# A decoder layer on one core: operands of the norm requested earlier, the second phase's pools in another order, the gate's finished rows two steps apart

## The chip, the cores and the metric

The kernel runs on one core of one Trainium2 chip. The metric is device microseconds of one execution, from its first to its last instruction with what lies around them; less is better. Engines are called as the profile calls them: PE (TensorE), DVE (VectorE), ACT (ScalarE), POOL (GpSimd), SP (SyncE, which here only issues transfers).

## The reference, cut to what matters

One decoder layer over 2048 tokens of width 1024, all in float32:

```python
u = _rmsnorm(h, ln1_g); proj = u @ w_in               # 3088 columns
...                                                   # gated linear attention, short convolution
h = h + concatenate([o, y]) @ w_out
u2 = _rmsnorm(h, ln2_g)
a, bb = split(u2 @ w_gate_upffn)                      # 2 x 2816 columns
h = h + (silu(a) * bb) @ w_down
u3 = _rmsnorm(h, ln3_g)
gate = sigmoid(u3 @ w_ple_gate)                       # 1024 x 1024
h = h + gate * (p @ w_ple_proj)                       # p: 2048 x 256, the embeddings
return _rmsnorm(h, lnf_g)
```

## The kernel before, in words

A float32 product is three fast matmuls: each operand is split into a rounded high part (a cast on ACT, L105 or L162) and a rest (a subtraction on DVE, L106 or L163), and high x high, high x rest and rest x high are summed. The three large products with `w_gate_upffn`, `w_down` and `w_ple_gate` are cut into blocks and made with seven block products in place of eight; the left operands of the seven are sums and differences of a first and a second half of the tokens' operands. They lie in DRAM as `up_1` to `up_7`, `u3_1` to `u3_7` and `hid_1` to `hid_7`.

There are three phases, each with pools of its own on the same SBUF addresses, given out in the order in which the pools are named. A tile of the next phase that lies where a tile of the phase before lay waits for the last use of that one.

- **Mixing phase** (0 to about 957 us): four blocks `b` of 512 tokens, each of `NT` = 4 tiles of 128 tokens. Only the order of PE's work is written by hand; the other engines' order is set by a scheduler. Near the end of a block each tile gets its residual, is stored (`h_mid<-w`, L670), normed (`normed`), transposed and written out by `norm_to_ops`. In blocks 0 and 2 this writes `up_1` and `up_2`. In blocks 1 and 3 (tile >= NT) it reads those two back (`old`, two loads, L232), makes four differences on POOL (L218, 128x512 each) and stores `up_3` to `up_7` (L235). After block 3 the embeddings of the first two blocks are multiplied with `w_ple_proj` (`embedding`): ACT copies the results (L725) and POOL issues their stores (`emb<-w`, L727).
- **Up phase** (to about 1870 us), order by hand. It opens with two loads of the other embeddings `p` (`ur<-in_p_dram`, L865), two of `w_ple_proj` (L869), splits them, turns `p` on PE (L267), and makes 16 embedding products (matmuls `mm<-U,U`, their stores L903) before the up product starts. Beside these, `fetch_U` loads the first `up_` operands (L280) and L790 the first weights. The SP queue runs its transfers in order; a transfer whose tile isn't free holds up all behind it.
- **Last phase**: the down product twice, then the gate for the first half of the tokens, `gated(0)`, and for the second, `gated(1)`, which is final. A step is twelve matmuls of 512 columns; `then(n, fn)` runs `fn` n steps later. A job is two steps; its two loads (`wr`, `mr`, L1023) are issued some jobs ahead, and its casts `wh`, `mh` (L162) two ahead. In `gated(0)` a finished row of 128 tokens goes through `finish`: POOL adds the residual with an accumulating transfer (`h<-h_out`, L1251), ACT squares it into a tile of the pool `w4` (L1107), POOL makes the inverse root, DVE scales (L1126) into the same tile, SP stores it (`out_dram<-w`, L1247). `w4` has four tiles here, so that the fifth row's squares wait until the first row's store has landed. ACT runs in order too: what waits there holds up the casts behind it. These steps of the eight rows of `gated(0)` fall into the first ones of `gated(1)`, whose own rows are loaded meanwhile (`row`, `h<-h_out` on SP, L1231).

Of the kernel before, what the change touches and what calls it, by code (L numbers as in the profile page):

```python
# [14 lines left out]
P = 128  # L15
# [4 lines left out]
NT = T // P  # L20
# [19 lines left out]
def hybrid_layer(ctx: ExitStack, tc: tile.TileContext,  # L40
                 x, p, ln1_g, w_in, w_gate_up, b_gate, conv_w, gn_g, w_out, ln2_g,
                 w_up, w_down, ln3_g, w_pg, w_pp, lnf_g, out):
    nc = tc.nc
    x, out = x[0], out[0]
# [9 lines left out]
    def tile_of(tag):  # L54
        return lambda shape, dt=F32: pl[tag].tile(shape, dt, name=tag)

    big, w4, t2 = tile_of("uT"), tile_of("w4"), tile_of("t2")
# [6 lines left out]
    def pools(stack, spec, space=None):  # L64
        for tag, bufs in spec.items():
            kw = {} if space is None else {"space": space}
            pl[tag] = stack.enter_context(tc.tile_pool(name=tag, bufs=bufs, reuse_waits="tile", **kw))
# [70 lines left out]
    def later(n, fn):  # L138
        queue.append((clock[0] + n, fn))
        queue.sort(key=lambda e: e[0])  # L140
# [30 lines left out]
    def tok_of(ti):  # L171
        return slice(ti * P, (ti + 1) * P)
# [3 lines left out]
    def rstd_of(src, dst):  # L176

        ss = tiny.tile([P, 1], F32, name="ss")
        nc.scalar.activation(out=dst, in_=src, func=AF.Square, scale=1.0 / 32.0, accum_out=ss)
        ms = tiny.tile([P, 1], F32, name="ms")  # L180
        nc.gpsimd.tensor_scalar(out=ms, in0=ss, scalar1=EPS, scalar2=None, op0=ALU.add)
        rs = tiny.tile([P, 1], F32, name="rs")
        last["rs"] = nc.gpsimd.tensor_tensor(out=rs, in0=ms, in1=mhalf[:, 0:1], op=ALU.pow)
        return rs
# [8 lines left out]
    def normed(src, gain):  # L193
        xn = w4([P, D])
        rs = rstd_of(src, xn)
        nc.vector.scalar_tensor_tensor(out=xn, in0=src, scalar=rs, in1=gain, op0=ALU.mult, op1=ALU.mult)
        return xn

    def transposed(xn, kk):
        tp = tr_bank().rearrange("p (a b) -> p a b", b=P)  # L200
        for a in range(4):
            c = (kk * 4 + a) * P
            nc.tensor.transpose(out=tp[:, a, :], in_=xn[:, c:c + P], identity=ident)
        return tp
# [12 lines left out]
    def tensor(e, out, a, b, op):  # L217
        return e.tensor_tensor(out=out, in0=a, in1=b, op=op)  # L218

    def norm_to_ops(src, tile, ops, gain, delay):  # L220

        xn = normed(src, gain)

        def transposes():
            tok = tok_of(tile % NT)
            ut = w4([P, 2, 4, P])
            if tile >= NT:
                old = w4([P, 2, 4, P])  # L230
                for kk in range(2):
                    nc.sync.dma_start(out=old[:, kk], in_=ops[1 + kk][:, :, tok])  # L232
            for kk in range(2):
                nc.scalar.copy(out=ut[:, kk], in_=transposed(xn, kk))
            put = lambda n, t: nc.sync.dma_start(out=ops[n][:, :, tok], in_=t)  # L235
            if tile < NT:
                put(1, ut[:, 0])
                put(2, ut[:, 1])
                return
            put(3, ut[:, 1])  # L240
            s = w4([P, 2, 4, P])
            g = nc.gpsimd
            tensor(g, s[:, 0], ut[:, 0], old[:, 0], ALU.subtract)
            put(5, s[:, 0])
            tensor(g, s[:, 1], ut[:, 1], s[:, 0], ALU.subtract)
            put(6, s[:, 1])
            tensor(g, ut[:, 0], ut[:, 1], ut[:, 0], ALU.subtract)
            put(7, ut[:, 0])
            tensor(g, old[:, 1], old[:, 1], s[:, 1], ALU.subtract)
            put(4, old[:, 1])  # L250
        later(delay, transposes)

    def load_x(b, ti, eng, gate=None):
# [511 lines left out]
    wp_view = w_pg.rearrange("(e i p) n -> p i e n", e=2, p=P)  # L765

    def up_phase(st):
        pools(st, {"raw": 6, "wu": 4, "v2": 12, "ur": 3, "U2": 3})
        pools(st, {"mm": 8}, bass.MemoryType.PSUM)
        V = nc.vector  # L770
        v2 = lambda: pl["v2"].tile([P, T], F32, name="v2")
# [91 lines left out]
        for q in range(EQ, NB):  # L863
            pts.append(pl["ur"].tile([P, 2, T], F32, name="ur"))
            nc.sync.dma_start(out=pts[-1].rearrange("p a t -> p (a t)").rearrange("p (t d) -> p t d", t=NT),  # L865
                              in_=p[q * T:(q + 1) * T, :].rearrange("(t p) d -> p t d", p=P))
# [121 lines left out]
    def last_phase(st):  # L988
# [58 lines left out]
        def then(n, fn):  # L1047
            order[0] += 1
            due.append((step[0] + n, order[0], fn))
# [56 lines left out]
        def squares(src, dst, ss):  # L1106
            nc.scalar.activation(out=dst, in_=src, func=AF.Square, scale=1.0 / 32.0, accum_out=ss)  # L1107

        def inverse(ss, more=0.0, name="rs"):
            ms = tiny.tile([P, 1], F32, name="ms")  # L1110
            nc.gpsimd.tensor_scalar(out=ms, in0=ss, scalar1=EPS, scalar2=more, op0=ALU.add, op1=ALU.add)
            rs = tiny.tile([P, 1], F32, name=name, bufs=4 if name == "rs" else 8)
            nc.gpsimd.tensor_tensor(out=rs, in0=ms, in1=mhalf[:, 0:1], op=ALU.pow)
            return rs

        def norm_steps(src, gain, start, gap, last_fn):

            got = {}

            def first():  # L1120
                got["xn"] = w4([P, D])
                got["ss"] = tiny.tile([P, 1], F32, name="ss8", bufs=8)
                squares(src, got["xn"], got["ss"])

            def scale():
                V.scalar_tensor_tensor(out=got["xn"], in0=src, scalar=got["rs"], in1=gain,  # L1126
                                       op0=ALU.mult, op1=ALU.mult)
            then(start, first)
            then(start + gap[0], lambda: got.update(rs=inverse(got["ss"])))
            then(start + gap[1], scale)  # L1130
            last_fn(got)
# [76 lines left out]
        def gated(b, lnf, final):  # L1208
# [3 lines left out]
            h = [None] * (2 * NT)  # L1212
# [3 lines left out]
            early, late = range(NT), range(NT, 2 * NT)  # L1216
# [10 lines left out]
            def row(t):  # L1227
                if h[t] is None:
                    h[t] = pl["h"].tile([P, D], F32, name="h")
                    if final:  # L1230
                        nc.sync.dma_start(out=h[t], in_=h_out[b * 2 * NT + t])  # L1231
                return h[t]

            def sigmoid(z, sg):
                nc.scalar.activation(out=sg, in_=z, func=AF.Sigmoid)

            def onto(t, cols, sg):

                if not final:
                    tensor(V, row(t)[:, cols], sg, pp[t, cols.start], ALU.mult)  # L1240
                    return
                tensor(V, sg, sg, pp[t, cols.start], ALU.mult)
                tensor(V, h[t][:, cols], h[t][:, cols], sg, ALU.add)

            def store(t, xo):
                r = b * BT + t * P
                nc.sync.dma_start(out=out[r:r + P, :], in_=xo)  # L1247

            def finish(t, start):
                def residual():  # L1250
                    nc.gpsimd.dma_start(out=h[t], in_=h_out[b * 2 * NT + t], accum_op=ALU.add)  # L1251
                then(start, residual)
                norm_steps(h[t], lnf, start + 4, (1, 2), lambda got: then(start + 7, lambda: store(t, got["xn"])))

            def early_half(t, cols):

# [6 lines left out]
            def late_squares(t, cols):  # L1263
                sq = pl["as"].tile([P, 2, 4, P], F32, name="as")
                ss = tiny.tile([P, 1], F32, name="ss8", bufs=8)
                squares(h[t][:, cols], sq[:, 0].rearrange("p a b -> p (a b)"), ss)
                late_rs[t] = inverse(ss, part[t], "rs8")
# [36 lines left out]
            def late_rows(t):  # L1304
                sigmoid(u2[t], u2[t])
                onto(NT + t, lo, u2[t])

            def done3(t, x):
                z = u2[t]
                tensor(V, z, x, z, ALU.add)  # L1310
                if final:
                    if t > 0:
                        late_rows(t - 1)
                    if t > 1:
                        late_squares(NT + t - 2, lo)
                    return
                then(1, lambda: sigmoid(z, z))
                then(2, lambda: onto(NT + t, lo, z))
                then(2, lambda: finish(NT + t, 1 + t))

            def done4(t, x):
                z = v("acc")
                sigmoid(x, z)
                then(1, lambda: onto(t, hi, z))
                then(1, lambda: finish(t, 2 + t))

            def last_done4(t, x):

# [19 lines left out]
            go = lambda n, on, done, **kw: stream(1, b, n, bk, on, done, **kw)  # L1348
            if final:
                for t in range(2 * NT):  # L1350
                    then(8 + t // 2 * 2, lambda t=t: row(t))
            then(1, lambda: fetch(early, lo, "pp"))
            go(1, None, done1)
            go(2, None, done2)
# [15 lines left out]
        g3, lnf = gain_of(ln3_g[0]), gain_of(lnf_g)  # L1370
# [3 lines left out]
        for b in range(NBB):  # L1374
            down(b, g3)
        gated(0, lnf, False)
        gated(1, lnf, True)


# [42 lines left out]
```

## Time and profile before

| what | before |
|---|---|
| time, median of 3 runs | 2488.64 us (2488.27 to 2496.26) |
| the profiled execution: its time | 2492.06 us |
| its span, first to last instruction | 2490.3 us |
| mean granted clock of PE | 0.983 |
| PE busy | 2380.4 us (96%) |
| DVE, ACT, POOL busy | 1394.1, 974.7, 698.6 us |
| moved by transfers | 471.08 MB, 189 GB/s over the span |

The profiled execution lies 3.4 us above the median, and 1.8 us of its time lie outside its span. In a timeline, a row gives start and duration of a run of like instructions, and in brackets how long the engine was idle before it and what released it. A row of windows gives for a stretch each engine's busy time with its number of instructions, then PE's granted clock, the busy share of the transfer engines (a full one can read slightly over 1) and GB/s.

### The profile page before, as it was taken

The page shows a single profiled execution, that of the slowest core. Times are in us where ns is not written, and L with a number is a line of the kernel's source. Part 1 is how long each engine was busy: PE and PEld are TensorE (multiplying, and loading weights), DVE is VectorE, ACT ScalarE, POOL GpSimd, SP SyncE. Part 2 cuts the span into 40 slices and gives each one's busy share as a digit, 9 for nine tenths or more (in the row PEclk, how much of TensorE's full clock was granted, in tenths as well). Part 3 has the DMA queues.
Part 4 walks back from the last instruction along what each step waited for, and adds up shares of the span by engine and source line. Part 5 has one row for each costly group of instructions (what it writes and reads, how often), then busy time and mean ns, then how long its engine had stood idle before and what let it go on. Part 6 is the DMA issues. An engine that isn't in the chain of part 4 may idle for free.

```text
span 2490.3 us, 31389 instructions
## 1 busy us (share of the span) xinstructions
PE 2380.4 (96%) x11752; PEld 1946.6 (78%) x11752; DVE 1394.1 (56%) x1676; ACT 974.7 (39%) x1533; POOL 698.6 (28%) x604
## 2 busy tenths in 40 slices
PE   7999999899999996999999999999999999999976
PEld 6777878777887784788888888888887888788765
DVE  4656465556646641655555664445546555655758
ACT  4434433443344333522222332222224344435555
POOL 3301210431103014244343243244522105301421
PEclk9999999999999997999999999999999999999988
DMA  4226323731542248854354576557757669756997
GB/s 154 68 68 217 103 72 135 217 99 59 170 153 68 68 145 274 277 175 164 135 181 162 196 260 217 202 200 256 259 203 288 201 220 296 276 189 239 330 298 273
DMA packets 274761, 471.08 MB, mean 189 GB/s; under 512 B 22688, under 2 KB 146096, under 8 KB 274608
## 3 DMA queue, kind: packets, MB, share of 16 engines
q1 hardware_dynamic: 272112, 460.66, 54.8%
q0 software_dynamic: 2496, 8.41, 1.4%
q8 instruction: 92, 1.51, 0.2%
q14 instruction: 61, 0.50, 0.1%
HBM read 326.92 MB, written 142.08 MB: 188 GB/s over the span
## 4 chain that ended last, share of the span: by engine, by line
PE 64%; DMA 7%; issue 3%; DVE 3%; ACT 2%; POOL 2%; SPq 0%; POOLq 0%; ACTq 0%; DVEq 0%
PE mm L148 46%; PE ps L1069 15%; DMA ur<-up 1%; DMA mr<-hid 1%; DMA mr<-u 1%; PE g L427 1%; DMA out_dram<-w 1%; POOL as L218 1%; DMA h<-h_out 1%; DMA w<-up 1%; POOL w L218 0%; DMA emb<-w 0%; DVE hl L106 0%; ACT mh L162 0%; PE ps L1102 0%
## 5 line engine op out<-in xcount | busy, mean ns | idle before, releaser
L1069 PE MATMUL ps<-wh,mh 128*128 128x512 f32 x2496 | 578.1, 392 | 23.2 <-ACT mh L162 16.0
L1069 PEld LDWEIGHTS ps<-wh,mh 128*128 128x128 f32 x2496 | 468.7, 189 | 126.3 <-ACT mh L162 18.0
L148 PE MATMUL mm<-uT,hl 128*128 128x512 f32 x1920 | 481.7, 405 | 10.1 <-DVE hl L106 6.3
L148 PE MATMUL mm<-uT,wu 128*128 128x512 f32 x2112 | 482.3, 389 | 0.0
L148 PEld LDWEIGHTS mm<-uT,wu 128*128 128x128 f32 x2112 | 396.5, 188 | 82.2
L148 PEld LDWEIGHTS mm<-uT,hl 128*128 128x128 f32 x1920 | 356.5, 190 | 105.1 <-DVE hl L106 11.8
L148 PE MATMUL mm<-U,wu 128*128 128x512 f32 x1584 | 364.5, 390 | 3.1 <-DVE v L218 3.1
L148 PEld LDWEIGHTS mm<-U,wu 128*128 128x128 f32 x1584 | 298.5, 188 | 65.6 <-issue 3.5
L163 DVE TENSOR_TENSOR wu<-raw,wu 128x1024 fp32r<-128x1024 f32 x154 | 218.1, 1416 | 209.3 <-ACT wu L162 208.8
L148 PE MATMUL mm<-hl,uT 128*128 128x512 f32 (+1 forms) x1584 | 301.0, 349 | 3.4 <-DVE uT L163 2.1
L148 PEld LDWEIGHTS mm<-hl,uT 128*128 128x128 f32 x1584 | 252.1, 190 | 42.8 <-DVE uT L163 2.7
L162 ACT CAST wu<-raw 128x1024 fp32r<-128x1024 f32 x154 | 161.5, 1050 | 304.7 <-PE mm L148 222.1
L163 DVE TENSOR_TENSOR wh<-wr,wh 128x1024 fp32r<-128x1024 f32 x111 | 141.3, 1273 | 235.8 <-ACT wh L162 235.0
L218 DVE TENSOR_TENSOR v<-mm,v 128x512 f32<-128x512 f32 x220 | 150.9, 687 | 151.4 <-PE mm L148 150.6
L218 POOL TENSOR_TENSOR v<-v,v 128x512 f32<-128x512 f32 x88 | 137.5, 1563 | 302.4 <-DMA hid<-v 262.0
L162 ACT CAST wh<-wr 128x1024 fp32r<-128x1024 f32 x111 | 110.8, 998 | 248.3 <-PE ps L1069 185.5
L106 DVE TENSOR_TENSOR hl<-raw,hl 128x512 fp32r<-128x512 f32 (+1 forms) x260 | 183.6, 744 | 26.5 <-ACT hl L105 26.3
L105 ACT CAST hl<-raw 128x512 fp32r<-128x512 f32 (+1 forms) x260 | 153.8, 622 | 61.3 <-PE mm L148 30.3
L218 POOL TENSOR_TENSOR raw<-raw 128x1024 f32<-128x1024 f32 x44 | 107.4, 2451 | 224.7 <-issue 149.3
L163 DVE TENSOR_TENSOR mh<-mr,mh 128x1024 fp32r<-128x1024 f32 x111 | 144.2, 1299 | 5.7 <-ACT mh L162 5.2
L162 ACT CAST mh<-mr 128x1024 fp32r<-128x1024 f32 x111 | 110.6, 996 | 9.4 <-DMA mr<-hid 7.2
L218 POOL TENSOR_TENSOR ur<-ur 128x512 f32<-128x512 f32 x60 | 93.5, 1559 | 31.7 <-DMA ur<-in_w_ple_gate_dram 26.9
(190 smaller groups left out, 1882.6 us busy)
## 6 DMA issues: line engine op xcount, KB each, us to landing
raw<-in_w_gate_upffn_dram SPq DMA_DIRECT2D x77, 512.0 KB, 4.8
hid<-v SPq DMA_DIRECT2D x154, 256.0 KB, 3.4
mr<-hid SPq DMA_DIRECT2D x70, 512.0 KB, 4.8
raw<-in_w_in_dram SPq DMA_DIRECT2D x64, 512.0 KB, 4.4
wu<-raw SPq DMA_DIRECT2D x44, 512.0 KB, 3.0
raw<-wu SPq DMA_DIRECT2D x44, 512.0 KB, 5.8
wr<-wd SPq DMA_DIRECT2D x40, 512.0 KB, 3.7
w<-in_x_dram SPq DMA_DIRECT2D x32, 512.0 KB, 9.0
```

Of the source, the lines that this page charges most:

```text
L105: nc.scalar.copy(out=hl[:, 0, :], in_=raw)
L106: nc.vector.tensor_tensor(out=hl[:, 1, :], in0=raw, in1=hl[:, 0, :].bitcast(F32), op=ALU.subtract)
L148: nc.tensor.matmul(out=out_ap, lhsT=lhs(k, a), rhs=rhs(k, b), start=(start and k == 0 and i == 0), stop=(k == nk - 1 and i == 2), **kw)
L162: nc.scalar.copy(out=hi, in_=src)
L163: nc.vector.tensor_tensor(out=lo, in0=src, in1=hi.bitcast(F32), op=ALU.subtract)
L218: return e.tensor_tensor(out=out, in0=a, in1=b, op=op)
L427: nc.tensor.matmul(out=sp[par][:, a, :], lhsT=X[r, c], rhs=X[r, c], start=True, stop=True)
L1069: nc.tensor.matmul(out=bk[n][t], lhsT=M[a][:, j, tok_of(t)], rhs=W[c][:, j, :], start=(on is None and k == 0 and i == 0), stop=(k == nk - ...
```

## The change

It has three parts. `norm_to_ops` allocates `old` and issues its two loads right after the norm and no longer just ahead of the transposed copies. The up phase names its pools in the order `ur`, `raw`, `v2`, `U2`, `wu`, so that other tiles lie at each address. In the gate, rows finish two steps apart in each of the two groups of four, the second group from step 5 on and no longer from 2; the store comes 8 steps after the row's start and not 7; and the eight rows of `gated(1)` are loaded at other steps (`gated(0)` only allocates its rows at step 9 in an order written out).

```diff
         xn = normed(src, gain)
+        tok = tok_of(tile % NT)
+        old = w4([P, 2, 4, P]) if tile >= NT else None
+        if tile >= NT:
+            for kk in range(2):
+                nc.sync.dma_start(out=old[:, kk], in_=ops[1 + kk][:, :, tok])
 
         def transposes():
-            tok = tok_of(tile % NT)
             ut = w4([P, 2, 4, P])
-            if tile >= NT:
-                old = w4([P, 2, 4, P])
-                for kk in range(2):
-                    nc.sync.dma_start(out=old[:, kk], in_=ops[1 + kk][:, :, tok])
...
-        pools(st, {"raw": 6, "wu": 4, "v2": 12, "ur": 3, "U2": 3})
+        pools(st, {"ur": 3, "raw": 6, "v2": 12, "U2": 3, "wu": 4})
...
-                norm_steps(h[t], lnf, start + 4, (1, 2), lambda got: then(start + 7, lambda: store(t, got["xn"])))
+                norm_steps(h[t], lnf, start + 4, (1, 2), lambda got: then(start + 8, lambda: store(t, got["xn"])))
...
-                then(2, lambda: finish(NT + t, 1 + t))
+                then(2, lambda: finish(NT + t, 1 + 2 * t))
...
-                then(1, lambda: finish(t, 2 + t))
+                then(1, lambda: finish(t, 5 + 2 * t))
...
-                    then(8 + t // 2 * 2, lambda t=t: row(t))
+                    then((7, 7, 8, 8, 10, 12, 14, 15)[t], lambda t=t: row(t))
+            else:
+                then(9, lambda: [row(t) for t in [*late, *early]])
```

The engines' order of instructions changes at three places.

SP at the end of the mixing phase. Before, `old` of the four tiles of block 3 (L232, from `up_1` and `up_2`) stands in front of each tile's stores, and the loads of `p` (L865) stand behind the last of them:

```order
L670 DMA h_mid_82<-w_7568 128x1024
L670 DMA h_mid_83<-w_7570 128x1024
L670 DMA h_mid_84<-w_7572 128x1024
L232 DMA w_7899<-up_1_109 128x4x128
L232 DMA w_7899<-up_2_111 128x4x128
L235 DMA up_3_114<-w_7898 512x1x128
...
L232 DMA w_8047<-up_1_109 128x4x128
L232 DMA w_8047<-up_2_111 128x4x128
...
L235 DMA up_4_115<-w_8047 512x1x128
L865 DMA ur<-in_p_dram 128x4x256 x2
L869 DMA raw<-in_w_ple_proj_dram 128x2x512 x2
```

After, the same engine and place (`old` is now L229):

```order
L865 DMA ur<-in_p_dram 128x4x256
L98 DMA raw<-in_w_out_dram 128x2x512
...
L865 DMA ur<-in_p_dram 128x4x256
L98 DMA raw<-in_w_ple_proj_dram 128x2x512
L670 DMA h_mid_82<-w_7568 128x1024
L229 DMA w_7783<-up_1_109 128x4x128
L229 DMA w_7783<-up_2_111 128x4x128
L670 DMA h_mid_83<-w_7570 128x1024
L229 DMA w_7852<-up_1_109 128x4x128
L229 DMA w_7852<-up_2_111 128x4x128
L670 DMA h_mid_84<-w_7572 128x1024
L229 DMA w_7904<-up_1_109 128x4x128
```

Both loads of `p` moved ahead of all stores of block 3, and the `old` of three tiles ahead of the first tile's stores.

SP at the end of block 1: the last two tiles' `old` (L232), their stores (L235) and weights (`in_w_in`, L98). Before:

```order
L98 DMA raw<-in_w_in_dram 128x2x512 x2
L670 DMA h_mid_77<-w_3732 128x1024
L232 DMA w_4195<-up_1_102 128x4x128
L232 DMA w_4195<-up_2_104 128x4x128
L235 DMA up_3_107<-w_4194 512x1x128
L98 DMA raw<-in_w_in_dram 128x2x512
L235 DMA up_5_105<-w_4211 512x1x128
...
L235 DMA up_4_108<-w_4195 512x1x128
L232 DMA w_4313<-up_1_102 128x4x128
```

After:

```order
L98 DMA raw<-in_w_in_dram 128x2x512 x2
L670 DMA h_mid_77<-w_3732 128x1024
L229 DMA w_4197<-up_1_102 128x4x128
L229 DMA w_4197<-up_2_104 128x4x128
L235 DMA up_3_107<-w_4200 512x1x128
L235 DMA up_5_105<-w_4214 512x1x128
...
L235 DMA up_4_108<-w_4122 512x1x128
...
L235 DMA up_4_108<-w_4197 512x1x128
L98 DMA raw<-in_w_in_dram 128x2x512
```

The last tile's `old` moved ahead of the stores of the tile before it, and one load of weights moved from among these behind all of them. The two loads of weights at the top keep their place behind the stores of the second tile.

SP in `gated(1)`: stores of the finished rows (L1247), loads of rows (L1231) and of the products' operands (L1023). Before:

```order
L1023 DMA mr<-u_5_126 128x1024
L1247 DMA out_dram<-w_18299 128x1024
L1247 DMA out_dram<-w_18329 128x1024
L1023 DMA wr<-wp_193 128x1024
L1023 DMA mr<-u_5_126 128x1024
L1247 DMA out_dram<-w_18358 128x1024
L1247 DMA out_dram<-w_18394 128x1024
L1231 DMA h<-h_out_94 128x1024
L1231 DMA h<-h_out_95 128x1024
L1023 DMA wr<-wp_192 128x1024
L1023 DMA mr<-u_7_127 128x1024
L1247 DMA out_dram<-w_18416 128x1024
```

After:

```order
L1023 DMA mr<-u_5_126 128x1024
L1247 DMA out_dram<-w_18297 128x1024
L1023 DMA wr<-wp_193 128x1024
L1023 DMA mr<-u_5_126 128x1024
L1231 DMA h<-h_out_94 128x1024
L1231 DMA h<-h_out_95 128x1024
L1247 DMA out_dram<-w_18348 128x1024
L1231 DMA h<-h_out_96 128x1024
L1231 DMA h<-h_out_97 128x1024
L1023 DMA wr<-wp_192 128x1024
L1023 DMA mr<-u_7_127 128x1024
L1247 DMA out_dram<-w_18397 128x1024
```

No two stores stand next to each other any more, and the rows' loads moved up among them. On ACT the squares of a row stand behind the casts of later jobs than before, two steps apart.

## The prediction

> **What bounds the kernel now.** The page first:
>
> ```profile
> PE 2380.4 (96%) x11752; PEld 1946.6 (78%) x11752; DVE 1394.1 (56%) x1676; ACT 974.7 (39%) x1533; POOL 698.6 (28%) x604
> ```
>
> PE is busy for 2380.4 of 2490.3 us and no other engine for over 56%, so what can be won without taking work from PE lies in its 110 us of holes. Next the windows of 20 us, where the places that the change touches show theirs:
>
> ```profile
> 940.00:960.00 20.00, 16.41 (x71) 12.85 (x69) 0.00 (x0) 7.32 (x13) 13.84 (x12) 1.00 0.85 254
> 960.00:980.00 20.00, 3.12 (x14) 2.75 (x15) 0.00 (x0) 0.00 (x0) 5.61 (x9) 0.53 0.93 309
> 480.00:500.00 20.00, 15.54 (x106) 15.09 (x105) 2.79 (x6) 4.85 (x12) 9.79 (x10) 0.83 0.87 263
> 2400.00:2420.00 20.00, 6.54 (x20) 4.57 (x19) 6.50 (x8) 7.02 (x12) 3.41 (x6) 0.66 0.85 302
> ```
>
> After the duration come PE's busy time with its count, PEld, DVE, ACT, POOL, the granted clock, the transfers' share and GB/s. At 960 (phase 1 to 2), 480 (end of block 1) and 2400 (gate) PE stands and its clock falls with it. What ended these holes is in PE's timeline:
>
> ```profile
> 939.30 17.11 PE L148 MATMUL mm<-hl,uT 128*128 128x512 f32 x72
> 970.89 1.94 PE L267 MATMUL mm<-ident,ur 128*128 128x128 f32 x8 [14.48 <-DMA ur<-in_p_dram]
> 978.82 1.97 PE L267 MATMUL mm<-ident,ur 128*128 128x128 f32 x8 [5.99 <-DMA ur<-in_p_dram]
> 983.38 1.22 PE L148 MATMUL mm<-U,U 128*128 128x512 f32 x2 [2.59 <-ACT U L162]
> 984.75 23.42 PE L148 MATMUL mm<-U,U 128*128 128x512 f32 x94 [0.15 <-DVE U L163]
> ```
>
> **Part one and two: the junction of the phases.** PE ends the mixing phase at 939.30 + 17.11 = 956.41 and runs its products from 984.75: 28.3 us, of which 23.2 are idle and 5.1 work. The loads of `p` came late because of SP, and SP because of POOL:
>
> ```profile
> 955.25 7.78 SPq L235 DMA_DIRECT2D up<-w  x5
> 963.08 11.44 SPq L865 DMA_DIRECT2D ur<-in_p_dram  x2
> 974.57 1.04 SPq L869 DMA_DIRECT2D raw<-in_w_ple_proj_dram  x2
> SPq L865 <- DMA emb<-w: 10.3, 1, 10.3
> ...
> 929.74 2.65 POOL L218 TENSOR_TENSOR w<-w,w 128x512 f32<-128x512 f32 x2 [2.04 <-DVE hl L106]
> 957.44 2.60 POOL L218 TENSOR_TENSOR w<-w,w 128x512 f32<-128x512 f32 x2 [5.18 <-DMA w<-up]
> 962.43 2.66 POOL L727 DMA_DIRECT2D emb<-w  x5
> ```
>
> The L865 row shows SP standing 10.3 us for the landing of an embedding store (the row of waits); these stores stand on POOL behind the last differences, and those waited 5.18 us for `old`. The new order of pools puts the tiles of `p` elsewhere and its loads among the weights of `w_out`, ahead of all stores of block 3, so PE's turns (2 x 1.95 us) can follow the last product directly. Requested with the norm, `old` of the first three tiles is asked for ahead of the first stores; POOL then needs 16 differences of 1.3 us, 21 us, from about 929.7, with small work between: the last ends near 951.5, not at 962.4. The loads of `w_ple_proj` (L869) follow at about 952, not 974.57. What is late next: the turned `p` is cast into a tile that now lies where the last embedding results lay. PE's last product ends at 956.41, its copy (first row below) at 957.0, and POOL can issue the store near 957.5. How such stores land stands in the line below its group (least, median, most):
>
> ```profile
> 956.45 0.58 ACT L725 COPY w<-mm 128x512 f32<-128x512 f32 x1 [0.81 <-PE mm L148]
> L727 POOL DMA_DIRECT2D emb<-w x8: 531/531/680, 945.5 to 965.1; - x8
> DMA to landing us min/median/max: 3.1/7.0/10.2
> 982.75 2.04 ACT L162 CAST U<-mm 128x512 fp32r<-128x512 f32 x4
> 1008.01 21.92 PE L148 MATMUL mm<-uT,wu 128*128 128x512 f32 x96
> 1860.00:1880.00 20.00, 17.86 (x75) 13.58 (x75) 8.55 (x8) 7.34 (x8) 2.36 (x2) 1.00 0.91 336
> ```
>
> With the median of 7.0 it lands at 964.5. From the first cast (982.75) to the steady matmuls (984.75) it took 2.0 us, so the products start near 966.5 and not at 984.75: 18 us. I take off 2 for what then comes closer together: the `up` operands and weights behind them, 4 MB that are asked for from 952 on and share the transfers with these stores (share 0.93 at 960 already). Term: -16 us. Ends: with the longest landing, 10.2, and 3 us of stalls it is -12; with the shortest, 3.1, and none, -22. The clock gives nothing here: some 8 us of standing remain, and the matmuls behind the old hole took 23.42 us for 94 where later ones took 21.92 for 96; that is paid in both. The pools' order also sets which tiles of the last phase wait at its start; PE's hole there is 2.1 us (the row of 1860), nothing in the order says that it grows or goes: 0, between -2 and +2.
>
> **Part one at the end of block 1.** The same waits, smaller:
>
> ```profile
> 474.64 6.09 PE L148 MATMUL mm<-hl,uT 128*128 128x264 f32 x48
> 484.24 1.97 PE L203 MATMUL tr<-ident,w 128*128 128x128 f32 x8 [3.51 <-ACT w L234]
> 485.86 5.14 PE L148 MATMUL mm<-hl,uT 128*128 128x264 f32 x24
> 470.87 3.25 POOL L218 TENSOR_TENSOR w<-w,w 128x512 f32<-128x512 f32 x2 [3.20 <-DMA w<-up]
> 478.17 1.11 SPq L98 DMA_DIRECT2D raw<-in_w_in_dram  x2
> 485.30 0.63 SPq L98 DMA_DIRECT2D raw<-in_w_in_dram  x1
> 483.08 0.62 ACT L105 CAST hl<-raw 128x512 fp32r<-128x512 f32 x1 [2.47 <-DMA raw<-in_w_in_dram]
> 504.56 0.62 ACT L105 CAST hl<-raw 128x512 fp32r<-128x512 f32 x1
> raw<-in_w_in_dram SPq DMA_DIRECT2D x64, 512.0 KB, 4.4
> ```
>
> POOL waits 3.20 for `old`; SP's stores wait for POOL, the two weights behind them go out at 478.17, their cast at 483.08 holds ACT, and the copies of the transposes behind it end PE's 3.51. The 24 matmuls after it ran slow: 5.14 against half of 6.09, 2.1 lost. Without the 3.20 the weights leave as much earlier and nearly all of the 5.6 goes. Against it, one load of weights that left at 485.30 now stands behind all stores of the last tile, near 498; if it is among those cast from 504.56 on, that covers its landing (4.4 at the median) as long as those stores aren't late. Tile 7's squares on ACT also wait now for two stores of tile 4 to land. Term: -3, between -6 and +4 (a late load holding PE for as long as the old hole).
>
> **Part three: the gate.**
>
> ```profile
> 2414.47 1.22 PE L1069 MATMUL ps<-wh,mh 128*128 128x512 f32 x2 [13.23 <-ACT mh L162]
> 2411.39 1.06 ACT L1107 ACTIVATE w<-h 128x1024 f32<-128x1024 f32 x1 [17.97 <-DMA out_dram<-w]
> 2392.63 3.51 SPq L1247 DMA_DIRECT2D out_dram<-w  x2
> DMA to landing us min/median/max: 3.0/8.4/18.7
> h<-h_out POOLq DMA_DIRECT2D x8, 512.0 KB, 14.3
> 2390.00:2400.00 10.00, 10.00 (x46) 8.29 (x45) 4.75 (x4) 3.21 (x6) 4.36 (x5) 1.00 1.07 246
> 2410.00:2420.00 10.00, 5.30 (x14) 3.87 (x15) 6.50 (x8) 7.02 (x12) 3.41 (x6) 0.56 0.67 242
> 2440.00:2450.00 10.00, 9.65 (x43) 7.66 (x41) 6.59 (x8) 4.22 (x4) 0.00 (x0) 1.00 1.03 406
> ```
>
> ACT stands 17.97 us for the first row's store (issued 2392.63, the 18.7 of the third line, which is that of the eight stores here); the casts behind it are what PE misses for 13.23. So 4.7 us of the wait were covered by casts made ahead. The change puts three steps between a store and the squares that reuse its tile, where it was one: two steps more, at 2.74 us each (12 matmuls at 21.92 / 96) 5.5 us. With the same landing the hole shrinks from 13.2 to 7.7; and fewer accumulating transfers are ahead of that store, as the rows come every second step. But the transfers are full (1.07 at 2390, 1.03 at 2440), and only about 3.3 us of them stand idle in the hole (0.67); what ACT no longer misses, the loads of operands may. Term: -6, between 0 (all 13 come back as late `mr`) and -14 (the hole and the slow clock after it).
>
> **Sum.** -16 - 3 - 6 = -25. The profiled execution, 2492.06 us (2490.3 of span, 1.8 around it), would come to 2467.1; it lies 3.4 above the median, and against the median of 2488.64 the forecast is 2463.6 us.
>
> **The rivals.** (a) Embedding stores and the burst of 4 MB hold the first casts or the first operands: junction -9 in place of -16, 2470.6. For it speaks the share of 0.93 there; against it, that fewer stores are then under way. (b) The gate stays bound by transfers: its term is 0, 2469.6. The row for it is 2390, where a share of 1.07 moves only 246 GB/s, against 406 at 2440, with accumulating transfers from POOL under way; these now lie over a longer stretch, beside more loads of operands. The Trainium skill, "DMA: Bandwidth & Descriptors", section "Queues, rings and completion order", says that each transfer engine takes packets from its queue rows in turn; by it a load on SP's queue goes at a shared pace as long as any of POOL's is under way, which is this rival; the trace agrees so far that loads of `h<-h_out` on POOL take 14.3 us at the median. (c) The gate's hole closes wholly, -13, as the spread stores land in time: 2456.6. (d) The change doesn't do what it says at the junction: a tile under `p` or `w_ple_proj` is still released by a late store, so only -9 remains of all, 2479.6. (e) Slower: the first cast of phase two waits for the last embedding store. If SP's burst is ahead of it and it lands more than 34 us after 957.5 (984.75 - 2.0 + 9 for the other terms, so at 992), all is lost; at 40 us the time is 2494. The longest landing there was 10.2, so little speaks for it.
>
> **How the numbers follow.** Forecast 0.50 (own range 2457 to 2469), (a) 0.13, (b) 0.13, (c) 0.12, (d) 0.08, (e) 0.04. A measurement here can tell about 0.3%, 7.5 us, from no change: below 2481.2 is faster. (e) is slower, and half of (d), which lies 1.6 us under that bound, no change: faster 0.92, same 0.04, slower 0.04. The range 2452 to 2475 takes in (a), (b) and (c) and the ends of the junction (-12 to -22) one at a time.
>
> **What would show it.** In the profile after: L865 on SP among the loads of `w_out`; POOL's L218 without `<-DMA w<-up`; the turns L267 right behind PE's last product and the first `mm<-U,U` near 966, released by ACT's cast with `emb<-w` behind it; no 3.51 at 484 and 24 matmuls of 264 columns in about 3 us; in the gate ACT's wait for `out_dram` under 12 us. I am wrong if PE's hole at the junction is over 20 us still, if one appears near 504 for the moved weights, or if PE waits in the gate for `mr<-u` itself for as long as it did for ACT.

## The result and the profile after

The changed kernel takes 2465.72 us (median of 4, 2461.07 to 2467.16) where the kernel before takes 2489.24 (median of 4, 2488.27 to 2496.26): ratio 0.9896, with a 95% interval of 0.9874 to 0.9919. It is 23.5 us faster, and the time lies 2.1 us above the forecast.

The profiled execution of after is its shortest one, 2461.07 us with a span of 2459.4; that of before lay 2.8 above its own median. So the two profiles differ by 31.0 us, 7.5 more than the medians. First the page of after, the line of busy times:

```profile
PE 2373.1 (96%) x11752; PEld 1941.7 (79%) x11752; DVE 1397.8 (57%) x1676; ACT 975.6 (40%) x1533; POOL 705.7 (29%) x604
```

The counts are those of before: no work went, only idle time and slow clock. PE is busy 7.3 us less with the same matmuls, at a mean granted clock of 0.990 where it was 0.983.

**The junction.** The timeline of after, of PE first:

```profile
944.61 2.98 PE L148 MATMUL mm<-hl,uT 128*128 128x512 f32 x12
947.43 1.91 PE L267 MATMUL mm<-ident,ur 128*128 128x128 f32 x16
962.37 1.22 PE L148 MATMUL mm<-U,U 128*128 128x512 f32 x2 [13.03 <-ACT U L162]
963.75 23.75 PE L148 MATMUL mm<-U,U 128*128 128x512 f32 x94 [0.15 <-DVE U L163]
987.33 21.92 PE L148 MATMUL mm<-uT,wu 128*128 128x512 f32 x96
```

The same timeline of SP, then POOL, then ACT:

```profile
886.49 0.37 SPq L865 DMA_DIRECT2D ur<-in_p_dram  x1
...
928.67 16.18 SPq L235 DMA_DIRECT2D up<-w  x15
944.90 2.34 SPq L869 DMA_DIRECT2D raw<-in_w_ple_proj_dram  x2
...
942.59 1.30 POOL L218 TENSOR_TENSOR w<-w,w 128x512 f32<-128x512 f32 x1
943.83 2.66 POOL L727 DMA_DIRECT2D emb<-w  x5
948.51 0.53 POOL L727 DMA_DIRECT2D emb<-w  x1 [2.02 <-ACT w L725]
...
959.46 1.04 ACT L162 CAST U<-raw 128x1024 fp32r<-128x1024 f32 x1 [11.24 <-DMA raw<-in_w_ple_proj_dram]
```

The turns of `p` (16 in one row) follow the last mixing product without a gap, `p` having been loaded 60 us earlier. From the end of that product (944.61 + 2.98 = 947.59) to the steady embedding products at 963.75 it takes 16.2 us, where it took 28.3: -12.2. To the first up product it is 39.7 us against 51.6: -11.9. What is left is one wait, 13.03 us of PE for ACT, and ACT's 11.24 are for the loads of `w_ple_proj`. They leave at 944.90, before PE is done, but land late. How long they took stands below their group (least, median, most), in before:

```profile
DMA to landing us min/median/max: 5.5/6.1/6.6
```

In after:

```profile
DMA to landing us min/median/max: 14.5/14.7/14.8
```

And the windows of after:

```profile
940.00:950.00 10.00, 9.34 (x49) 7.58 (x47) 0.00 (x0) 3.52 (x6) 7.00 (x10) 1.00 1.02 325
950.00:960.00 10.00, 0.00 (x0) 0.00 (x0) 0.00 (x0) 0.54 (x1) 0.00 (x0) 0.74 1.03 376
```

These two say why a reader should suspect the transfers: from 940 to 960 their share is full (1.02, 1.03), and from 950 no engine computes anything but one cast.

**The end of block 1.** The timeline of after, four rows of PE and one of SP:

```profile
474.98 6.09 PE L148 MATMUL mm<-hl,uT 128*128 128x264 f32 x48
482.26 1.13 PE L203 MATMUL tr<-ident,w 128*128 128x128 f32 x8 [1.19 <-ACT w L234]
483.14 3.19 PE L148 MATMUL mm<-hl,uT 128*128 128x264 f32 x24
510.93 16.66 PE L148 MATMUL mm<-uT,hl 128*128 128x512 f32 x69
493.39 11.34 SPq L98 DMA_DIRECT2D raw<-in_w_in_dram  x11
```

The hole of 3.51 is now 1.19, the transposes behind it take 1.13 in place of 1.97, and the 24 matmuls 3.19 in place of 5.14. From the row at 474.98 to that at 510.93 it is 35.95 us; in before the same two rows start at 474.64 and 516.72, 42.08 apart: -6.1. A hole of 0.96 behind the 24 matmuls of before is gone as well. The granted clock of the stretch behind the hole was 0.55 in before (484.24 to 491) and is 1.00 now (482.26 to 488). The weight that was moved is in the last row, behind all stores, and no hole stands near it.

**The gate.** PE's timeline, of before at first, where the stretch begins and its last product:

```profile
2334.74 16.20 PE L1069 MATMUL ps<-wh,mh 128*128 128x512 f32 x70 [1.72 <-DVE mh L163]
2468.84 1.52 PE L1069 MATMUL ps<-wr,mr 128*128 128x512 f32 x6
```

Then of after, with two rows of ACT behind those of PE:

```profile
2311.34 16.87 PE L1069 MATMUL ps<-wh,mh 128*128 128x512 f32 x72 [1.72 <-DVE mh L163]
2379.80 0.73 PE L1069 MATMUL ps<-wh,mh 128*128 128x512 f32 x2 [2.25 <-ACT mh L162]
2399.93 0.73 PE L1069 MATMUL ps<-wh,mh 128*128 128x512 f32 x2 [1.08 <-ACT mh L162]
2435.83 1.52 PE L1069 MATMUL ps<-wr,mr 128*128 128x512 f32 x6
...
2375.84 1.05 ACT L162 CAST wh<-wr 128x1024 fp32r<-128x1024 f32 x1 [7.73 <-DMA wr<-wp]
2391.27 1.06 ACT L1107 ACTIVATE w<-h 128x1024 f32<-128x1024 f32 x1 [2.37 <-DMA out_dram<-w]
```

The accumulating transfers of after between 2340 and 2450 (issues, size, median us to landing):

```profile
h<-h_out POOLq DMA_DIRECT2D x8, 512.0 KB, 8.7
```

And, of after, the stretch of work that the prediction quoted at 2390 to 2400 of before; after comes to it 23.4 us earlier (2334.74 less 2311.34):

```profile
2366.60:2376.60 10.00, 10.00 (x46) 8.29 (x45) 2.42 (x2) 2.27 (x4) 2.53 (x3) 1.00 1.06 301
```

From behind the hole of 1.72, which both kernels have, to PE's last product it took 135.6 us before (2334.74 to 2468.84 + 1.52) and takes 126.0 now. ACT's wait for a store fell from 17.97 to 2.37, and the hole of 13.23 became two of 2.25 and 1.08 and some of about half a microsecond. What ACT waits for most is now a load of operands (7.73 for `wr`). The accumulating transfers land in 8.7 us at the median where they took 14.3. Another wait went with these: between 2310 and 2470 SP stood 16.1 us in before (four times, 10.0 at most) for DVE to scale a row whose store was next in its order, with loads of operands behind it; in after it is 0.2.

Of the 9.6 us won here 2.1 are given back behind PE's end: the span ends 19.9 us after it before, 22.1 now. DVE's last `g<-ps,g` shows why, in the timeline of before:

```profile
2470.99 0.69 DVE L218 TENSOR_TENSOR g<-ps,g 128x512 f32<-128x512 f32 x1
```

In after:

```profile
2440.02 0.68 DVE L218 TENSOR_TENSOR g<-ps,g 128x512 f32<-128x512 f32 x1
```

Before it started 0.6 us behind PE's end (2470.36), now 2.7 behind it (2437.35): DVE has a queue of work there, and PE's earlier end doesn't bring that forward in full.

**The account** of the two profiles: junction -11.9, block 1 -6.1, gate -9.6 and +2.1; -2.7 in the rest of the mixing phase and -2.7 in the up and down products. Neither is put down to the change: old_and_pools and U2_ahead below, whose mixing phase is the same as after's, end it at 950.15 and 950.56, about 3 us later, and over the kernels below the up and down products, which the change doesn't touch, differ by up to 6 us. Sum -31. Without the last two it is -25.5, beside -23.5 of the medians.

### The profile page after: what moved, and what is told of

Same layout as the page of the kernel before. It is cut to its first block, busy times and chain, and to the rows that moved or that the text cites. A ratio compares the mean times of both kernels' runs of the same rounds, so it can differ in the third digit from the quotient of the medians.

```text
span 2459.4 us, 31386 instructions
## 1 busy us (share of the span) xinstructions
PE 2373.1 (96%) x11752; PEld 1941.7 (79%) x11752; DVE 1397.8 (57%) x1676; ACT 975.6 (40%) x1533; POOL 705.7 (29%) x604
```

## The experiments

The first four kernels hold parts of the change. The theory was that the two queues act one after the other at the junction, POOL's late differences first and the order of the pools second; the rivals gave the gain to one of them.

**old_only**: the first hunk of the change alone (`old` loaded right behind the norm).

> Only the operands of norm_to_ops are requested with the norm; pools and gate as before. Theory: at the junction two queues stood in series, POOL's late differences and SP's late loads of p, and each part takes away one. Then this alone gives the whole of block 1 (-6 us) and at the junction some -8 (28.3 us from the last embedding matmul to the products become about 20), since the loads of p still stand behind the stores and wait for an embedding store: about 2475 us. Rival 1, POOL's differences were the whole cause: the junction comes to the 16 us of the changed kernel, total -18, 2471. Rival 2, the pools' order was the whole cause: block 1 alone, -6, 2483.

Measured: 2475.57 (5 runs), ratio 0.9930 (0.9914 to 0.9945). PE's timeline there:

```profile
965.12 1.94 PE L267 MATMUL mm<-ident,ur 128*128 128x128 f32 x8 [10.01 <-DMA ur<-in_p_dram]
973.46 22.78 PE L148 MATMUL mm<-U,U 128*128 128x512 f32 x94 [0.15 <-DVE U L163]
```

SP's wait (sum, times, longest):

```profile
SPq L865 <- DMA emb<-w: 9.7, 1, 9.7
```

SP still stands 9.7 us for an embedding store, but the last differences, and with them this store, come sooner. The junction takes 18.3 us in place of 28.3 (-10.0), and block 1 is shorter by 5.5 with a hole of 1.81. So this part alone has most of both gains, as the theory of two queues expected.

**pools_only**: the pools in the new order alone.

> Only the pools of the up phase are named in the new order. Theory of two queues in series: p is there in time, but the loads of w_ple_proj leave behind the differences near 963 and the last embedding store lands near 974, so that the products start near 976 and not at 984.75: -8 us, about 2481. Rival 1 (POOL's differences were the whole cause): 0, 2489. Rival 2 (the pools' order was): -12, 2477. Block 1 keeps its hole of 3.5 in all.

Measured: 2488.99 (11 runs), ratio 0.9986 (0.9975 to 0.9996), that is 3.5 us. The timeline of PE, SP and POOL:

```profile
956.52 1.91 PE L267 MATMUL mm<-ident,ur 128*128 128x128 f32 x16
980.74 9.53 PE L148 MATMUL mm<-U,U 128*128 128x512 f32 x31 [22.31 <-ACT U L162]
963.96 1.89 SPq L869 DMA_DIRECT2D raw<-in_w_ple_proj_dram  x2
958.32 2.60 POOL L218 TENSOR_TENSOR w<-w,w 128x512 f32<-128x512 f32 x2 [5.79 <-DMA w<-up]
```

The turns come at once, as in after, but then PE stands 22.31: the loads of `w_ple_proj` leave at 963.96, behind the stores of the last differences, which wait for `old` as before. The junction takes 24.1 us, 4.3 less than in before, where 8 were expected. Removing SP's wait for `p` only showed the next one; the rival that held POOL's late differences for the main cause comes nearer.

**old_and_pools**: both, without the gate's part.

> The first two parts together, the gate as before. If the parts add up with the gate, this is the changed kernel without its gate: -6 in block 1 and -12 at the junction, about 2471, and the gate keeps its 13 us hole. If the gate's hole depends on what goes before, it differs from the changed kernel by another amount than the gate alone gives.

Measured: 2473.84 (5 runs), ratio 0.9922 (0.9908 to 0.9937). The junction takes 16.8 us, 1.6 less than with `old` alone. The gate keeps its hole (12.88).

**gate_only**: the gate's part alone.

> Only the gate's rows are spaced. Theory: the 13.2 us hole goes, some 5 to 6 us of small holes come in its place as the transfers are full, -7 us: 2482. Rival, the gain seen in the gate of the changed kernel's profile is that execution's luck (it lies 5 us under the other three): -2 or less, 2487.

Measured: 2482.08 (6 runs), ratio 0.9956 (0.9940 to 0.9971); from the hole of 1.72 to PE's end 126.4 us, with 22.0 behind it, as in after. ACT's waits there (sum, times, longest):

```profile
ACT w L1107 <- DMA out_dram<-w: 3.8, 3, 3.3
ACT wh L162 <- DMA wr<-wp: 14.1, 5, 6.3
```

Within the intervals the parts multiply: 0.9930, 0.9986 and 0.9956 give 0.9872, and the whole is at 0.9896. At the junction the first two overlap: 10.0 and 4.3 us alone, 11.6 together. The gate's part adds less in the last step (0.9922 to 0.9896) than alone, but the intervals overlap.

**squares_apart**: before, with the squares of a finished row written into another pool (`as`), and a tile of `w4` taken only by the scaling two steps later. The rows follow each other as in before, so this lengthens the distance from store to reuse to three steps without spreading the accumulating transfers.

```diff
             def first():
-                got["xn"] = w4([P, D])
+                dst = pl["as"].tile([P, 2, 4, P], F32, name="as")... if apart else w4([P, D])
+                got["xn"] = None if apart else dst
                 ...
-                squares(src, got["xn"], got["ss"])
+                squares(src, dst, got["ss"])
             def scale():
+                if apart:
+                    got["xn"] = w4([P, D])
```

> The kernel before, but in the gate the squares of a finished row go into a tile of another pool (as), and the tile of w4 is taken only by the scaling two steps later; rows finish one step apart as before. The distance from store to reuse becomes 3 steps without any spreading. If the distance is what counts, the hole of 13.2 us falls to about 7.7 and the time by 5 to 6 us, as the arithmetic of the prediction had it for landings that stay at 18.7. Rival: the spreading counts (accumulating transfers no longer in one heap); then DVE stands where ACT stood, the hole stays near 13 less a little, and the time within 2 us of before.

Measured: 2488.04 (11 runs), ratio 0.9988 (0.9978 to 0.9998). PE's timeline in the gate:

```profile
2404.69 8.30 PE L1069 MATMUL ps<-wh,mh 128*128 128x512 f32 x26 [6.79 <-ACT mh L162]
```

ACT's longest waits for transfers, and the accumulating transfers:

```profile
ACT wh L162 <- DMA wr<-wp: 22.6, 7, 9.4
```

```profile
h<-h_out POOLq DMA_DIRECT2D x8, 512.0 KB, 14.3
```

ACT doesn't wait for a store any more, and the hole halves to 6.79; behind it now stand loads of `wr`, and the accumulating transfers take 14.3 as before. From the hole of 1.72 to the end of the span it is 151.2 us, 155.6 before and 148.1 after: the distance alone brings 4.3 of the 7.5. The other three kernels with the old gate need 157.1 to 157.9 there, so it may be up to 6.7; the runs' ratio gives 3.0 us (0.5 to 5.5), where 5 to 6 were expected. The rest comes with the other edits of the gate's part. No kernel here tells apart what does it: the accumulating transfers that land sooner, SP's waits for scalings (16.1 us before, 7.5 here, 0.2 after), or the loads of `gated(1)`'s rows, which were moved too.

**gate_stores_early**: after, without the eight stores of finished rows of the first half of the tokens; block 2 of the mixing phase stores as many bytes of other data to those addresses long before, so half of its output is not the layer's. This asks whether the gate's remaining holes are transfers.

```diff
+                            if b == 2:
+                                for r in (2 * ti, 2 * ti + 1):
+                                    nc.sync.dma_start(out=out[r * P:(r + 1) * P, :], in_=h[ti])
...
-                norm_steps(..., lambda got: then(start + 8, lambda: store(t, got["xn"])))
+                norm_steps(..., lambda got: None)
```

> The changed kernel without the eight stores of the first gate's finished rows (4 MB): in their place block 2 of the mixing phase stores other data to these rows, so that the output there isn't the reference's. Theory: with the rows spaced the gate is bound by its transfers, so 4 MB less at some 380 GB/s, 11 us of them, take away all holes there (5 to 6 us): the time from 2330 us on falls from 130.7 us by 5 to 7, the total by as much if block 2 hides its stores. Rival: what is left in the gate are waits of engines for each other; then under 2 us.

Measured: 2458.26 (4 runs), ratio 0.9863 (0.9846 to 0.9879). PE's stretch (2318.14 to 2439.86 here) falls from 126.0 to 121.7 and what stands behind it from 22.1 to 19.2: -7.1 beside after, where 5 to 7 were expected. So the gate of after is held by what the transfers carry. ACT's last waits for stores, 2.9 us in all, go with the stores too; junction_and_gate below takes these away alone and gains nothing.

The next kernels take up the 13.03 that stay at the junction.

**U2_ahead**: after, with `U2` ahead of `v2` in the pools, so that the casts' tile does not lie on the last embedding results. If the landing of their store ends PE's wait, as the prediction had it, the wait must shrink.

> The changed kernel with U2 named ahead of v2 in the pools, so that the casts of the turned p lie on no tile of the embedding results; nothing else. Theory: at the junction of the changed kernel the loads of w_ple_proj, which land 14.7 us after they are issued, end PE's wait, and the embedding stores' landing is not it: the first product stays at 16 us after the last embedding matmul, and the time is the changed kernel's, 2466 (within 3 us). Rival (the prediction's step): the last embedding store ends it; then the gap falls by the 2 to 4 us that the store lands later than the loads, and the time to about 2462.

Measured: 2465.16 (4 runs), ratio 0.9900 (0.9886 to 0.9913), the same as after. ACT's timeline:

```profile
962.26 1.04 ACT L162 CAST U<-raw 128x1024 fp32r<-128x1024 f32 x1 [11.08 <-DMA raw<-in_w_ple_proj_dram]
```

The landing of the two loads:

```profile
DMA to landing us min/median/max: 14.2/14.2/14.3
```

The wait stays at 11.08, and so does the landing. The embedding store under the cast's tile isn't what ends it. It would not end much sooner, though: in after the last embedding store is issued at 948.51, and of the six from 943 on none takes over 10.7 us to land, so it is there by 959.2; ACT's cast of the first load starts at 959.46. Two waits end nearly together here. Had the loads been there in time, the store would by the prediction's path have let the products start near 961.2 (959.2 + 2.0) in place of 963.75; that is an estimate from these rows.

**emb_stores_early**: after, with six of the eight embedding stores (3 MB) made from the tiles of `p` when these are loaded, far ahead; the `emb` of those tiles then holds `p`. The loads of `w_ple_proj` keep their place and time.

```diff
+            for ti in range(2, EQ * NT):
+                nc.gpsimd.dma_start(out=emb[ti], in_=emb0["p"][ti // NT].rearrange("p t d -> p (t d)"))
...
-                nc.gpsimd.dma_start(out=emb[ti], in_=o)
+                if ti < 2:
+                    nc.gpsimd.dma_start(out=emb[ti], in_=o)
```

> The changed kernel, but the stores of six of the eight embedding tiles (3 MB) are made from the tiles of p, before the end of the mixing phase, when the transfers have room; what they store is not the embeddings. Theory: the loads of w_ple_proj are slow since POOL's stores share the transfers with SP's; without them they land in 10 us or less and not 14.7, and the products start about 5 us earlier, 2461. Rival: they stand behind SP's own stores of up; then the landing stays at 14 and the time at 2466.

Measured: 2458.25 (4 runs), ratio 0.9869 (0.9855 to 0.9882). The landing of the two loads, then PE's timeline:

```profile
DMA to landing us min/median/max: 6.5/6.6/6.6
```

```profile
957.19 1.22 PE L148 MATMUL mm<-U,U 128*128 128x512 f32 x2 [5.00 <-ACT U L162]
958.56 23.15 PE L148 MATMUL mm<-U,U 128*128 128x512 f32 x94 [0.15 <-DVE U L163]
```

POOL's queue between 935 and 960 (packets, MB, share of the transfer engines), in after:

```profile
q0 software_dynamic: 1094, 3.96, 43.6%
```

In this kernel:

```profile
q0 software_dynamic: 288, 1.05, 10.7%
```

With POOL's queue at 10.7% of the transfer engines in place of 43.6%, the same loads land in 6.6 us and not 14.7, though the transfers are as full as in after (1.00 and 1.02 between 940 and 960) and the 3 MB of loads on SP behind them are still there, as are SP's 15 stores of `up` ahead of them. The junction takes 8.1 us in place of 16.2. So 8 of the 13 us are shown to be the price of the embedding stores; 5.00 stay. This kernel has neither the traffic nor a late store under the cast's tile; U2_ahead, without the tile alone, kept the landing at 14.2, so that it is the stores' share of the transfers that makes the loads late. The parts of the change say the same: in old_only the loads leave at 963.52, behind the embedding stores, and land in 6.0, in old_and_pools in 14.8. The Trainium skill, "DMA: Bandwidth & Descriptors", section "Queues, rings and completion order", says that a transfer engine serves the queue rows that have work in turn, packet by packet; the landings agree with it, a load on SP's queue taking a little over twice as long (14.7 for 6.6) beside POOL's stores.

**first_half_early**: U2_ahead, with the first half of `w_ple_proj` loaded into a third tile of `ur`, which is free early, the embedding products made half by half, and the second half split after six of them.

```diff
+        wpp_raw = [... for t in (pl["ur"].tile([P, 2, T], F32, name="ur"), raw())]
...
+        cut_wpp(0)
...
-        for q in range(EQ, NB):
-            for ti in range(NT):
-                for n in range(2):
+        for n in range(2):
+            for q in range(EQ, NB):
+                for ti in range(NT):
+                    if u == 6:
+                        cut_wpp(1)
```

> As U2_ahead, and the first of the two loads of w_ple_proj lies in the third tile of ur, so that it is requested early, beside p; the 16 products are made first for the first half of the columns, and the second half is cut after six of them. If only the landing of w_ple_proj holds PE, the products start some 3 us after the last embedding matmul and not 16: -13 us, 2453. Rival: the transfers are full there (share 1.02 to 1.04 from 930 to 970), the operands of the first up product come no earlier, and PE waits for them at the end of the 16 products instead: some 0 to -4, 2462 to 2466.

Measured: 2458.83 (4 runs), ratio 0.9869 (0.9856 to 0.9883). It keeps the whole computation and has the lowest ratio of the kernels here that do, some 7 us below after, though the intervals of the two overlap a little. Three rows of PE's timeline and one of ACT's:

```profile
953.34 11.34 PE L148 MATMUL mm<-U,U 128*128 128x512 f32 x47 [0.28 <-DVE U L163]
968.84 0.80 PE L148 MATMUL mm<-U,U 128*128 128x512 f32 x1 [4.16 <-ACT U L162]
971.95 12.66 PE L148 MATMUL mm<-U,U 128*128 128x512 f32 x47 [2.31 <-DVE U L163]
962.83 1.07 ACT L904 COPY v<-mm 128x512 f32<-128x512 f32 x2 [7.07 <-DMA emb<-w]
```

The products start about 3 us behind the mixing phase, but PE stops in their middle for 4.16 and 2.31, and the first up product comes 34.0 us after the last mixing product, 5.8 sooner than in after; 13 was expected. ACT stands 7.07 for an embedding store here, since the copies' tiles (`v2`) lie where it is read.

**v2_last**: the same with `wu` ahead of `v2`, so that these copies lie elsewhere.

> As first_half_early, with wu ahead of v2 in the pools. In first_half_early ACT stood 7 us for an embedding store under the second result tile; now the result tiles lie under earlier embedding tiles, whose stores land sooner. If that wait held the products, their two stalls (4.2 and 2.3 us) shrink: -3 to -5, 2455. Rival: the operands behind them come no earlier, as the transfers are full, and the time stays at 2459.

Measured: 2461.69 (4 runs), ratio 0.9878 (0.9863 to 0.9893): no gain over first_half_early. PE, then ACT:

```profile
968.35 0.79 PE L148 MATMUL mm<-U,U 128*128 128x512 f32 x1 [4.17 <-ACT U L162]
963.52 1.05 ACT L162 CAST uT<-ur 128x1024 fp32r<-128x1024 f32 x1 [5.51 <-DMA ur<-up]
```

ACT's wait for the store, which ended at 962.83, is gone, but until 963.52 it now stands for the first `up` operand. PE's stops are the same to 0.01 us. The tile was not the limit: ACT's casts come in order, and the one that PE's stop needs stands behind that of an operand that is still on its way, on transfers that are full (1.07 between 960 and 970).

**junction_and_gate**: v2_last, with squares_apart on top of the spread rows.

> v2_last, and in the gate, with the rows spaced as in the changed kernel, the squares go into a tile of as, so that the reuse of a tile of w4 lies five steps behind its store. If ACT's waits for stores still cost the gate something, 2 us less than v2_last, near 2453; if it is bound by its transfers alone, v2_last's time.

Measured: 2463.4 (4 runs), ratio 0.9889 (0.9872 to 0.9906). ACT waits for no store in the gate any more, but the gate's stretch is 126.6 us with 21.9 behind it, the same as in v2_last: no gain. With rows spread, ACT's remaining waits for stores cost nothing that can be seen here, which fits a gate bound by its transfers.

## Why the prediction was right

The sum was right, and so were the places and, but for one at the junction, the waits; the terms were off in both directions: predicted -16, -3, -6, measured -12, -6, -7.5. That 4 us too much in the first and 4.5 too little in the other two cancel is luck.

- **`old` and POOL.** Right: no difference of block 3 waits for `old` any more, and the last of them ends 3.7 us ahead of PE's last mixing product (943.9 against 947.6; 4.9 ahead by the prediction's 951.5 and 956.41).
- **The order of the pools.** Right that the loads of `p` go out among the weights of `w_out` and that PE's turns follow directly. As a cause it is small: `old` alone gives 10.0 of the junction's 12.2, the order of the pools 4.3 alone and 1.6 on top of `old`.
- **What is late next at the junction.** This is the step that failed. The prediction had the loads of `w_ple_proj` follow and gave them no time to land, and took the last embedding store, through the tile it leaves, for what ends last. U2_ahead takes that tile out of the way and nothing changes. The loads themselves end it, at 14.7 us in place of the 6.1 of before, because the change brings them beside the embedding stores; emb_stores_early takes six of the eight stores away and has 6.6. The store that the prediction named was not much better: up to 10.7 us to land, not the median of 7.0. The 2 us taken off for what comes closer together should have been 6. The term is at the near end of its own range (-12) and nearer to rival (a), -9 with stores and burst holding the first casts, than to -16.
- **The clock** at the junction gave nothing, as said: 94 matmuls in 23.75 us behind the hole, against 23.42 before.
- **Block 1.** The mechanism was right, the size was not: -6.1 for -3. Of the 5.6 that were said to go, 4.3 went (2.32 of the hole, 1.95 of the slow matmuls); the slow transposes (0.84) and the hole of 0.96 behind the matmuls, which the prediction had not counted, make up the rest. The 2.6 held back for the moved weight were not needed: ACT waits 1.69 for a load of weights at 504.46, and PE has no hole there.
- **The gate.** Right that ACT's wait falls under 12 and that loads of operands take its place; -7.5 in all for -6. The prediction let the hole shrink only by the two steps, to 7.7. squares_apart, which has the distance alone, leaves 6.79, so that part was sized well. The prediction named that fewer accumulating transfers would be ahead of the store, but gave it no time; they land in 8.7 us for 14.3. That this makes the rest is argued and not shown, as squares_apart leaves open. Rival (b) had expected these transfers to be in the way over a longer stretch; the same stretch of work moves 301 GB/s at a share of 1.06 where it moved 246 at 1.07. That the gate is then bound by transfers, as the rival says, gate_stores_early shows: 7.1 us more without 4 MB of stores.
- **The slower case** (e) did not come near: the first steady embedding product starts 16.2 us after the mixing phase, not 28.3 or more.

Open is why the gate's part gives 0.9956 alone and 0.9922 to 0.9896 on top of the others. The profiles have it the other way round, 7.2 us alone (155.6 to 148.4 from the hole of 1.72 to the end) and 9.8 on top (157.9 to 148.1), and the runs' intervals allow both.

## What to carry to other kernels

When a hole closes, the transfers on both sides of it move together: a landing time read where they were apart isn't the one to use. The sign to lengthen it is another queue's stores at that place; the share of the transfers alone is not, as it was full with landings of 14.7 and of 6.6. A wait on a buffer and a wait on a crowded transfer can end at nearly the same time; move the buffer alone, and then the traffic alone. On an engine that runs in order, a tile that is reused one step after its store holds up all work behind; spreading the rows that use it lengthens that distance, and here the slowest transfers landed sooner as well.

## What was not expected of the hardware

A load of 512 KB on SP's queue landed in 14.7 us beside POOL's stores and in 6.6 without six of the eight, with the share of the transfers at 1.0 in both. Accumulating transfers of 512 KB landed in 14.3 us at the median when a row came every step and in 8.7 when it came every second one. Behind a wait of 3.51 us the 32 matmuls and transposes took 2.8 us more (1.97 and 5.14 against 1.13 and 3.19) at a granted clock of 0.55, nearly as much as the wait itself; at the same place they did not behind waits of 1.19 (after) and 1.81 (old_only), where the clock was 1.00.
